# Hybrid diffusion step on one core: the first modulation quarter is loaded right behind the first token tile, and a quarter's projections stand partly ahead of the next quarter's modulation

## The chip, the cores and the metric

The kernel runs on one core of one Trainium2 chip, in one launch. The metric is the device time of one execution in microseconds (us), the median of repeated runs; lower is better.

## The reference, cut to what matters

Two layers (DEPTH 2, D_MODEL 1024) run over 256 latent tokens and 128 context tokens. What matters here is how a layer begins: a conditioning vector is multiplied with a wide weight, the normalised tokens are scaled and shifted by pieces of the product, and one combined projection follows.

```
mod_ctx = (jax.nn.silu(c_ctx) @ w_mod[l] + b_mod[l])[None, :]
mod_lat = jax.nn.silu(c) @ w_mod[l] + b_mod[l]
...
sh1, sc1, g1, sh2, sc2, g2 = [m[:, None, :] for m in jnp.split(mod, 6, axis=-1)]
h = layer_norm(x) * (1 + sc1) + sh1
z = h @ p["w_in"] + p["b_in"]
q, k, v, conv_in, f_in, gates = jnp.split(z, SPLITS, axis=-1)
... attention, convolution and Fourier branches, merged by gates
x = layer_norm(ALPHA * x + g1 * (merged @ p["w_o"]), p["ln1_g"], p["ln1_b"])
... feed-forward with a depthwise convolution, second residual and norm
```

All of it is float32; the kernel keeps that accuracy by splitting an operand into a high and a low float32r part and adding three products.

## The kernel before

The 384 tokens are three tiles of 128: t0 and t1 latent, t2 context. The 1024 features are eight blocks of 128 (k).

**Start.** `run` sets up constants and a run of 30 products of zeros on PE (`busy`, L130), loads the three token tiles (`s`, 512 KB each) and the parameter rows (`par`), normalises the tiles on DVE (L327 and L329 statistics, L330 adds eps, POOL takes the root at L331, L336 applies it), and calls the layers.

**First layer, `start_first` (L415).** Modulation is done in four quarters s, each giving shift and scale for two k blocks. A quarter has two 1024 KB weight blocks (`raw<-w_mod`, L247). Its generator `mod` first loads them, then runs 32 small products in two groups of 16 (L232, 16 for each block), copies the result out of PSUM (L264, DVE), transposes it (L268, PE) and adds the bias into the columns `md` (L277, four small DVE instructions, for shift and scale of context and latents).

With `md` there, `to_hT` transposes two k blocks of each token tile (L356, PE) and applies scale and shift, one block on ACT (L365) and the other on DVE (L363); `split_hT` makes the high part on ACT (L371) and the low part on DVE (L372). The projection weight of the quarter (`s<-w_z`, two halves of 512 KB) is split by `halves` into `whi` on ACT (L178) and `wlo` on DVE (L179). `products` then runs 36 matmuls of 128x512 (L195 to L197): 2 halves, 3 token tiles, 2 k blocks, 3 products each, into six PSUM accumulators. Those of quarter s are traced after the transposes of quarter s + 1 (`late`, L436).

**What sets the order.** Each engine executes its own list in order. The lists are made by a scheduler from the traced program; buffers come from pools whose sizes are in `BUFS` (L80): among them 3 `raw`, 5 `whi`, 5 `wlo`, 8 `s4`, and two PSUM tiles `ps` (L119), which modulation and transposes share. All loads of this stage are issued by SP, on one queue. After `start_first` the convolution's input projection (L474, weights `raw<-w_cv`) begins.

Of the kernel before, what the change touches and what calls it, by code (L numbers as in the profile page):

```python
# [78 lines left out]
class Net:  # L79
# [46 lines left out]
    def busy(self, n):  # L126
        """products of zeros: they keep the tensor engine's clock up until the data is there"""
        ps = self.psum()
        for i in range(n):
            self.nc.tensor.matmul(ps[:, 0:P], self.zeros, self.zeros, start=i == 0, stop=i == n - 1)  # L130
# [39 lines left out]
    def halves(self, parts):  # L170
        """f32 half units -> their float32r (high, low) parts"""
# [11 lines left out]
    def raw(self, w):  # L183
        """one block [P, kn, 2048 // kn] of weights"""
        r = self.t("raw", [P, 2048]).rearrange("p (k c) -> p k c", k=w.shape[1])
        self.load(r, w)
        return r
# [5 lines left out]
    def mm3(self, ps, lh, ll, rh, rl, first, last):  # L193
        mm = self.nc.tensor.matmul
        mm(ps, lh, rh, start=first, stop=False)  # L195
        mm(ps, lh, rl, start=False, stop=False)  # L196
        mm(ps, ll, rh, start=False, stop=last)  # L197

    def ws_tile(self, hT, w, n=NTOK):
        """one 128-column tile of h @ w, features on partitions"""  # L200
# [6 lines left out]
    MODS = {"A": 0, "B": 1, "G": 2}  # L207

    def mod(self, l, kind, s=None):
        """c @ w_mod for the groups of a kind (A: sh1 sc1, B: sh2 sc2, G: g1 g2), or quarter s of them;  # L210
        a step per row tile"""
# [108 lines left out]
    def stats(self, src, w):  # L320
        """columns: mean, 1 / sqrt(var + eps)"""
# [16 lines left out]
    def norm_act(self, dst, src, total):  # L338
        """dst: src normalised, total: its rows' sums"""
# [9 lines left out]
    def to_hT(self, l, which, t, k0, nk, xhat, tag):  # L349
        """modulated transposes of row tiles k0.. of token tile t"""  # L350
# [64 lines left out]
    def start_first(self, l, xhat, hT, z):  # L415
        """first layer: a quarter of the modulation at a time, then what needs it"""
        acc = [[self.psum("acc") for _ in range(3)] for _ in range(2)]
        mods = [self.mod(l, "A", s) for s in range(4)]

        def loads(s):  # L420
            ws = [self.s4().rearrange("p (k c) -> p k c", k=2) for _ in range(2)]
# [4 lines left out]
        def products(s, raws):  # L426
            for half, (hi, lo) in enumerate(self.halves(raws)):
                for t in range(3):
# [6 lines left out]
        next(mods[0])  # L435
        late = None  # L436
        for s in range(4):
            for _ in mods[s]:
                pass
            raws = loads(s)  # L440
            if s < 3:
                next(mods[s + 1])
            for t in range(3):
                self.split_hT(t, 2 * s, 2, self.to_hT(l, 0, t, 2 * s, 2, xhat[t], "ps"), hT, 0)
            if late:
                products(*late)
            late = s, raws
        self.setup_late()
        bb = self.b_bias(l)
        products(*late)  # L450
# [114 lines left out]
    def fourier(self, f):  # L565
        """per channel tile the transform's transpose, split"""
# [33 lines left out]
    def rotate(self, dst, src, t, n):  # L600
        """dst, src: [P, n heads, 2, 32]"""
# [10 lines left out]
    def keys(self, l, z):  # L612
        """transposed keys (columns t0 t1 ctx prompt) of each kv head: high parts twice, low parts twice"""
# [146 lines left out]
    def close(self, acc, x, gate, lg, lb, last=None):  # L760
        """acc: the sub-layer's output for one token tile in two banks; returns the new x and its rows' sums"""
# [32 lines left out]
    def layer(self, l, first, hT, mods):  # L794
# [24 lines left out]
        # feed-forward: the first NF column tiles go by token tile, in plain float32  # L819
# [131 lines left out]
    def run(self):  # L951
        self.setup()
        xhat = [self.s4() for _ in range(3)]
        for t in range(3):
            self.load(xhat[t], self.x_src(0, t))
        self.columns(0)
# [17 lines left out]
def layout(i):  # L974
    """the inputs in the order in which the kernel loads them"""
# [4 lines left out]
    def cols(w, width=256):  # L980
        """[L, R, C] -> per block of columns [P, R / P, width]"""
# [3 lines left out]
    def rows(w, n=2):  # L985
        """[L, R, C] -> per n row tiles [P, n, C]"""
# [54 lines left out]
```

## Time and profile before

| | |
|---|---|
| median of 3 runs | 1193.04 us (1192.70 to 1194.32) |
| span of the profiled execution | 1190.3 us |
| around that span, by the median | 2.7 us |
| PE busy | 1170.9 us, 98% of the span |
| DVE, ACT, POOL busy | 754.0, 523.9, 76.4 us |

The profiled execution's span runs from its first to its last instruction; no other time is given for that execution, so what lies around it is taken as the median less the span. A busy PE is not PE at its peak: matmuls are pipelined, and the next one starts before the one ahead has ended.

### The profile page before, as it was taken

The numbers are of one execution on the slowest core, as the hardware profiler recorded it, in microseconds if no ns is written. First come the engines' busy times: TensorE is split into PE (matmuls) and PEld (weight loads), VectorE is DVE, ScalarE is ACT, GpSimd is POOL, SyncE is SP. The second block draws the span as 40 slices with busy tenths as digits, with TensorE's granted clock in tenths as the row PEclk, the third lists the DMA queues.
The fourth block names the chain that finished last, engine by engine and source line by source line (L and its number), as shares of the span: only waits on it lengthen the run. The fifth ranks groups of instructions, "written<-read, shape, count | busy, mean of one in ns | idle before, by whom it ended". The sixth has DMA issues, their size and how long they took to land.

```text
span 1190.3 us, 16806 instructions
## 1 busy us (share of the span) xinstructions
PE 1170.9 (98%) x6637; PEld 1023.5 (86%) x6637; DVE 754.0 (63%) x1269; ACT 523.9 (44%) x875; POOL 76.4 (6%) x91
## 2 busy tenths in 40 slices
PE   8999999999999999999999999999999999999996
PEld 6788788867899999999966887888989999999995
DVE  6569965424676665566685598653557666655668
ACT  3447643223464443444454566432427444443440
POOL 1010001111100000000011000011211000000001
PEclk9999999999999999999999999999999999999999
DMA  9655576674263333343425545775335343433311
GB/s 374 268 182 185 184 243 235 210 267 164 103 230 124 115 134 130 118 140 108 141 81 187 191 156 193 236 236 175 107 140 200 123 140 107 142 109 139 117 61 53
DMA packets 49791, 194.90 MB, mean 164 GB/s; under 512 B 5760, under 2 KB 6800, under 8 KB 34608
## 3 DMA queue, kind: packets, MB, share of 16 engines
q1 hardware_dynamic: 49280, 193.04, 46.8%
q8 instruction: 52, 0.85, 0.3%
q10 hardware_dynamic: 432, 0.79, 0.2%
q14 instruction: 27, 0.22, 0.1%
HBM read 190.37 MB, written 3.44 MB: 163 GB/s over the span
## 4 chain that ended last, share of the span: by engine, by line
PE 86%; DVE 6%; ACT 2%; DMA 2%; POOL 1%; issue 1%; SPq 0%; POOLq 0%; DVEq 0%; ACTq 0%
PE ps L195 17%; PE ps L196 16%; PE ps L197 16%; PE acc L195 9%; PE acc L196 9%; PE acc L197 8%; PE acc L232 4%; PE acc L716 1%; POOL sm L331 1%; PE acc L704 1%; DVE wlo L179 1%; DVE s L777 1%; DMA raw<-w_mod 1%; DVE sm L327 1%; DVE s L767 1%
## 5 line engine op out<-in xcount | busy, mean ns | idle before, releaser
L179 DVE TENSOR_TENSOR wlo<-raw,whi 128x1024 fp32r<-128x1024 f32 x216 | 269.9, 1251 | 278.7 <-ACT whi L178 278.6
L195 PE MATMUL ps<-hT,whi 128*128 128x386 f32 (+1 forms) x1088 | 372.6, 342 | 0.2 <-ACT g L503 0.2
L196 PE MATMUL ps<-hT,whi 128*128 128x386 f32 (+1 forms) x1088 | 369.1, 339 | 0.0
L197 PE MATMUL ps<-hT,wlo 128*128 128x386 f32 (+1 forms) x1088 | 368.9, 339 | 0.0
L178 ACT CAST whi<-raw 128x1024 fp32r<-128x1024 f32 x216 | 225.7, 1048 | 314.4 <-PE ps L196 217.8
L195 PEld LDWEIGHTS ps<-hT,whi 128*128 128x128 f32 x1088 | 205.2, 189 | 33.2 <-issue 20.3
L196 PEld LDWEIGHTS ps<-hT,whi 128*128 128x128 f32 x1088 | 205.2, 189 | 4.1 <-issue 3.2
L197 PEld LDWEIGHTS ps<-hT,wlo 128*128 128x128 f32 x1088 | 205.3, 189 | 2.7 <-issue 2.7
L196 PE MATMUL acc<-wlo,r 128*128 128x512 f32 x360 | 142.3, 395 | 0.0
L195 PE MATMUL acc<-whi,r 128*128 128x512 f32 x360 | 142.2, 395 | 0.0
L197 PE MATMUL acc<-whi,r 128*128 128x512 f32 x360 | 141.9, 394 | 0.0
L197 PEld LDWEIGHTS acc<-whi,r 128*128 128x128 f32 x360 | 67.6, 188 | 16.3 <-DVE r L899 0.5
L195 PEld LDWEIGHTS acc<-whi,r 128*128 128x128 f32 x360 | 67.6, 188 | 15.1
L196 PEld LDWEIGHTS acc<-wlo,r 128*128 128x128 f32 x360 | 67.6, 188 | 14.5
L734 DVE SCALAR_TENSOR_TENSOR cv<-upad,cst,cv 128x399 f32<-128x399 f32 x120 | 69.9, 625 | 0.1
L898 ACT CAST r<-g 128x386 fp32r<-128x386 f32 x44 | 22.7, 516 | 97.5 <-DVE g L896 97.5
L331 POOL TENSOR_TENSOR sm<-sm,mhalf 128x1 f32<-128x1 f32 x21 | 22.9, 1094 | 613.3 <-DVE sm L330 608.4
L518 POOL TENSOR_TENSOR g<-g,g 128x384 f32<-128x384 f32 x32 | 34.8, 1087 | 393.9 <-DVE g L517 389.7
L875 ACT ACTIVATE g<-ps,cst 128x386 f32<-128x386 f32 x84 | 56.3, 670 | 0.0
L232 PE MATMUL acc<-s,cpad 128*32 128x512 f32 x320 | 55.4, 604 | 0.7 <-DMA s<-w_mod 0.7
L878 DVE SCALAR_TENSOR_TENSOR g<-ps,cst,g 128x385 f32<-128x385 f32 x84 | 52.0, 620 | 2.8
L876 DVE SCALAR_TENSOR_TENSOR g<-ps,cst,g 128x385 f32<-128x385 f32 x84 | 51.6, 614 | 0.3
(184 smaller groups left out, 1314.6 us busy)
## 6 DMA issues: line engine op xcount, KB each, us to landing
raw<-w_u SPq DMA_DIRECT2D x44, 1024.0 KB, 5.0
s<-w_mod SPq DMA_DIRECT2D x160, 256.0 KB, 4.6
raw<-w_g SPq DMA_DIRECT2D x24, 1024.0 KB, 6.8
raw<-w_d SPq DMA_DIRECT2D x22, 1024.0 KB, 4.9
raw<-w_mod SPq DMA_DIRECT2D x8, 1024.0 KB, 12.4
raw<-w_o SPq DMA_DIRECT2D x8, 1024.0 KB, 7.8
s<-w_z SPq DMA_DIRECT2D x8, 512.0 KB, 11.0
raw<-w_cv SPq DMA_DIRECT2D x4, 1024.0 KB
```

The costliest lines, as they stand in the source:

```text
L178: self.nc.scalar.copy(hi, raw)
L179: self.nc.vector.tensor_tensor(lo, raw, f32(hi), op=ALU.subtract)
L195: mm(ps, lh, rh, start=first, stop=False)
L196: mm(ps, lh, rl, start=False, stop=False)
L197: mm(ps, ll, rh, start=False, stop=last)
L232: nc.tensor.matmul(ps[32 * i:32 * i + 32, 0:n], self.cpad[:, k, :], src[k, i], start=k == 0, stop=k == KD - 1)
L331: nc.gpsimd.tensor_tensor(mv[:, 3:4], mv[:, 2:3], self.mhalf, op=ALU.pow)
L518: nc.gpsimd.tensor_tensor(merged[m], merged[m], gt, op=ALU.add)
L734: nc.vector.scalar_tensor_tensor(c, u[:, i:i + CV_W], w, c, op0=ALU.mult, op1=ALU.add)
L875: nc.scalar.activation(c, ps, AF.Identity, bias=cols["ffn_b"][:, i:i + 1], scale=w[1])
L876: nc.vector.scalar_tensor_tensor(c[:, 1:NPAD], ps[:, 0:NPAD - 1], w[0], c[:, 1:NPAD], op0=ALU.mult, op1=ALU.add)
L878: nc.vector.scalar_tensor_tensor(c[:, 0:NPAD - 1], ps[:, 1:NPAD], w[2], c[:, 0:NPAD - 1], op0=ALU.mult, op1=ALU.add)
```

## The change

The first quarter's modulation weights are queued behind token tile t0 and ahead of `par`, the first half of `w_z`, tiles t1 and t2, and the second half of `w_z`. In `start_first` a quarter's weights are loaded ahead of its transposes, and its products are no longer held until the next quarter: the first token tile's products (for the first quarter, the first two tiles') stand ahead of the next quarter's modulation, and the others behind it. `issue_after` queues the PE instructions of the block under it behind the named matmul.

```diff
 def mm3(self, ps, lh, ll, rh, rl, first, last):
...
-        mm(ps, ll, rh, start=False, stop=last)
+        self.last_mm = mm(ps, ll, rh, start=False, stop=last)
...
 def start_first(self, l, xhat, hT, z):
...
-        next(mods[0])
-        late = None
-        for s in range(4):
+        def modulate(s):
             for _ in mods[s]:
                 pass
-            raws = loads(s)
+
+        raws = loads(0)
+        modulate(0)
+        for s in range(4):
             if s < 3:
                 next(mods[s + 1])
+                more = loads(s + 1)
             for t in range(3):
                 self.split_hT(t, 2 * s, 2, self.to_hT(l, 0, t, 2 * s, 2, xhat[t], "ps"), hT, 0)
-            if late:
-                products(*late)
-            late = s, raws
-        self.setup_late()
-        bb = self.b_bias(l)
-        products(*late)
+            ws = self.halves(raws)
+            cut = 1 if s else 2
+            products(s, ws, range(cut))
+            if s < 3:
+                with self.tc.issue_after(self.last_mm.ins):
+                    modulate(s + 1)
+                raws = more
+            else:
+                self.setup_late()
+                bb = self.b_bias(l)
+            products(s, ws, range(cut, 3))
...
 def run(self):
         self.setup()
         xhat = [self.s4() for _ in range(3)]
-        for t in range(3):
+        self.load(xhat[0], self.x_src(0, 0))
+        self.first_mods = [self.mod(0, "A", s) for s in range(4)]
+        next(self.first_mods[0])
+        self.columns(0)
+        self.first_w = [self.s4().rearrange("p (k c) -> p k c", k=2) for _ in range(2)]
+        self.load(self.first_w[0], self.a["w_z"][0, 0, 0])
+        for t in (1, 2):
             self.load(xhat[t], self.x_src(0, t))
-        self.columns(0)
+        self.load(self.first_w[1], self.a["w_z"][0, 1, 0])
```

**DVE, the first quarter.** Before: the rows around the copy of the first modulation product (L264); `s_120` is token tile t2, `s_221` and `s_222` the two halves of the first `w_z`.

```order
L330 TENSOR_SCALAR sm_160<-sm_160 128x1
L336 TENSOR_SCALAR s_120<-s_120,sm_160 128x1024
L264 COPY s_176<-ps_181 128x128
L277 TENSOR_TENSOR md_140<-ps_215,cst_131 128x2 x4
L179 TENSOR_TENSOR wlo_328<-s_221,whi_327 128x1024
L363 TENSOR_SCALAR s_233<-ps_230,md_140 128x128
```

All three tiles are normalised ahead of the copy there. In the changed program the same place reads as follows; `s_119` and `s_120` are tiles t1 and t2, `s_144` the first half of `w_z`.

```order
L179 TENSOR_TENSOR wlo_259<-s_144,whi_258 128x1024
L327 BN_STATS sm_158<-s_119 128x6 x2
L264 COPY s_122<-ps_185 128x128
L329 BN_AGGR sm_161<-sm_158 128x2
L327 BN_STATS sm_166<-s_120 128x6
L330 TENSOR_SCALAR sm_161<-sm_161 128x1
L327 BN_STATS sm_166<-s_120 128x6
L336 TENSOR_SCALAR s_119<-s_119,sm_161 128x1024
L329 BN_AGGR sm_169<-sm_166 128x2
L277 TENSOR_TENSOR md_143<-ps_219,cst_134 128x2
```

A weight split and two statistics now stand ahead of the copy, and the norms of two tiles between the copy and the columns. The list goes on:

```order
L277 TENSOR_TENSOR md_143<-ps_219,cst_134 128x2
L330 TENSOR_SCALAR sm_169<-sm_169 128x1
L277 TENSOR_TENSOR md_143<-ps_219,cst_134 128x2 x2
L336 TENSOR_SCALAR s_120<-s_120,sm_169 128x1024
L277 TENSOR_TENSOR md_143<-ps_219,cst_134 128x2
L179 TENSOR_TENSOR wlo_263<-s_145,whi_262 128x1024
L363 TENSOR_SCALAR s_237<-ps_234,md_143 128x128
```

The last of the four L277, which completes the columns, has moved behind the norm of t2.

**PE, from the first quarter to the second.** Before: the transposes of quarter 1 (L356 into `ps_303`, `ps_311`) stand between products of quarter 0.

```order
L268 MATMUL ps_288<-ident,s_225 128x128
L356 MATMUL ps_303<-ident,s_118 128x128 x2
L195 MATMUL acc_173<-whi_331,hT_165 128x512
L196 MATMUL acc_173<-wlo_332,hT_165 128x512
L197 MATMUL acc_173<-whi_331,hT_166 128x512
L356 MATMUL ps_311<-ident,s_119 128x128 x2
L195 MATMUL acc_173<-whi_331,hT_165 128x512
```

In the changed program all three pairs stand behind the last product of quarter 0, and the first product that needs them right behind.

```order
L195 MATMUL acc_184<-whi_262,hT_174 128x512
L196 MATMUL acc_184<-wlo_263,hT_174 128x512
L197 MATMUL acc_184<-whi_262,hT_175 128x512
L356 MATMUL ps_351<-ident,s_118 128x128 x2
L356 MATMUL ps_359<-ident,s_119 128x128 x2
L356 MATMUL ps_367<-ident,s_120 128x128 x2
L195 MATMUL acc_179<-whi_375,hT_174 128x512
```

No product of the old quarter is left to stand among the transposes; the same holds at the two later quarters.

**ACT, before the last quarter.** Before: `whi_612` and `whi_616` are the last quarter's `w_z`, `s_535` the first scaled block, `whi_683` a `w_cv` weight of the next stage.

```order
L178 CAST whi_612<-s_528 128x1024
L365 ACTIVATE s_535<-ps_532,md_140 128x128
L178 CAST whi_616<-s_529 128x1024
L365 ACTIVATE s_543<-ps_540,md_140 128x128
L371 CAST hT_165<-s_535 128x2x128
```

In the changed program three splits of the next stage's weights stand ahead of the last quarter's scaling.

```order
L178 CAST whi_683<-raw_681 128x1024
L178 CAST whi_687<-raw_681 128x1024
L178 CAST whi_839<-raw_837 128x1024
L365 ACTIVATE s_579<-ps_576,md_143 128x128
L365 ACTIVATE s_587<-ps_584,md_143 128x128
L371 CAST hT_174<-s_579 128x2x128
```

The first L365 of that quarter has moved behind `whi_839`, whose DVE part (L179) likewise stands ahead of the quarter's first L363.

## Rows read from the trace of the kernel before

**Rows 1.** The page, busy time and share of the span by engine.
```profile
PE 1170.9 (98%) x6637; PEld 1023.5 (86%) x6637; DVE 754.0 (63%) x1269; ACT 523.9 (44%) x875; POOL 76.4 (6%) x91
```
**Rows 2.** Busy time by stretches: stretch, length, then busy (count) by engine.
```profile
core 0: us, PE busy (x) PEld busy (x) DVE busy (x) ACT busy (x) POOL busy (x), PEclk, DMA share, GB/s
13.77:18.34 4.57, 2.48 (x40) 1.53 (x40) 3.64 (x10) 3.26 (x6) 0.00 (x0) 1.00 1.02 420
18.34:62.00 43.66, 43.66 (x362) 33.92 (x363) 25.72 (x54) 18.02 (x32) 3.13 (x6) 1.00 0.79 303
```
**Rows 3.** Timeline of the start: start, us, engine, instruction, idle before and releaser.
```profile
1.05 9.70 PE L130 MATMUL ps<-zeros 128*128 128x128 f32 x60 [1.05 <-DVE zeros L135]
4.75 0.69 DVE L327 BATCH_NORM_STATS2 sm<-s 128x6 f32<-128x512 f32 x1 [2.09 <-DMA s<-x_s]
...
8.72 2.08 DVE L336 TENSOR_SCALAR s<-s,sm 128x1024 f32<-128x1024 f32 x2
...
13.17 0.55 POOL L331 TENSOR_TENSOR sm<-sm,mhalf 128x1 f32<-128x1 f32 x1 [3.63 <-DVE sm L330]
13.75 0.81 DVE L336 TENSOR_SCALAR s<-s,sm 128x1024 f32<-128x1024 f32 x1 [0.66 <-POOL sm L331]
...
13.77 1.08 PE L232 MATMUL ps<-raw,cpad 128*32 128x128 f32 x32 [1.27 <-DMA raw<-w_mod]
...
14.92 0.29 DVE L264 COPY s<-ps 128x128 f32<-128x128 f32 x1 [0.36 <-PE ps L232]
15.03 1.04 ACT L178 CAST whi<-s 128x1024 fp32r<-128x1024 f32 x1 [10.94 <-DMA s<-w_z]
...
15.63 0.36 DVE L277 TENSOR_TENSOR md<-ps,cst 128x2 f32<-128x2 f32 x4 [0.42 <-PE ps L268]
...
16.11 1.23 DVE L179 TENSOR_TENSOR wlo<-s,whi 128x1024 fp32r<-128x1024 f32 x1
...
17.25 0.72 DVE L363 TENSOR_SCALAR s<-ps,md 128x128 f32<-128x128 f32 x2
...
17.88 0.40 ACT L371 CAST hT<-s 128x256 fp32r<-128x256 f32 x1
...
18.34 0.50 PE L195 MATMUL acc<-whi,hT 128*128 128x512 f32 x1 [0.18 <-ACT hT L371]
```
**Rows 4.** Timeline of quarter 2: DVE waits while work behind its head is ready.
```profile
31.60 1.05 ACT L178 CAST whi<-s 128x1024 fp32r<-128x1024 f32 x1 [1.31 <-DMA s<-w_z]
...
34.45 0.29 DVE L264 COPY s<-ps 128x128 f32<-128x128 f32 x1 [3.67 <-PE ps L232]
...
35.70 1.21 DVE L179 TENSOR_TENSOR wlo<-s,whi 128x1024 fp32r<-128x1024 f32 x1
```
**Rows 5.** Timeline of quarter 2: transposes among products, and the scaling behind them.
```profile
35.22 0.38 PE L356 MATMUL ps<-ident,s 128*128 128x128 f32 x2
35.36 0.48 PE L196 MATMUL acc<-wlo,hT 128*128 128x512 f32 x1
...
35.88 0.46 ACT L365 ACTIVATE s<-ps,md 128x128 f32<-128x128 f32 x1 [3.23 <-DVE md L277]
```
**Rows 6.** Timeline of PE around one group of modulation products.
```profile
32.98 0.39 PE L195 MATMUL acc<-whi,hT 128*128 128x512 f32 x1
33.30 1.08 PE L232 MATMUL ps<-raw,cpad 128*32 128x128 f32 x32
34.31 0.51 PE L196 MATMUL acc<-wlo,hT 128*128 128x512 f32 x1
34.65 0.39 PE L197 MATMUL acc<-whi,hT 128*128 128x512 f32 x1
34.88 0.39 PE L195 MATMUL acc<-whi,hT 128*128 128x512 f32 x1
```
**Rows 7.** Busy time by stretches, the products of zeros and the end of PE's work.
```profile
1.05:4.00 2.95, 2.95 (x14) 2.95 (x15) 0.21 (x1) 1.50 (x2) 0.51 (x2) 1.00 0.55 167
6.80:10.60 3.80, 3.80 (x35) 3.76 (x34) 3.73 (x8) 0.00 (x0) 1.90 (x4) 1.00 1.05 428
1180.00:1185.00 5.00, 1.12 (x5) 0.57 (x3) 4.62 (x9) 0.00 (x0) 0.65 (x1) 0.94 0.28 105
```

More of the change, by code (lines that the diff above doesn't have):

```diff
@@ L417, in start_first @@
         acc = [[self.psum("acc") for _ in range(3)] for _ in range(2)]
-        mods = [self.mod(l, "A", s) for s in range(4)]
+        mods = self.first_mods
         def loads(s):
+            if s == 0:
+                return self.first_w
             ws = [self.s4().rearrange("p (k c) -> p k c", k=2) for _ in range(2)]
@@ L424, in loads, with products @@
             return ws
-        def products(s, raws):
-            for half, (hi, lo) in enumerate(self.halves(raws)):
-                for t in range(3):
+        def products(s, ws, tiles):
+            for half, (hi, lo) in enumerate(ws):
+                for t in tiles:
                     ts = slice(t * P, t * P + P)
@@ L953, in run @@
         xhat = [self.s4() for _ in range(3)]
-        for t in range(3):
+        self.load(xhat[0], self.x_src(0, 0))
[5 more added lines that the diff above has]
+        for t in (1, 2):
             self.load(xhat[t], self.x_src(0, t))
-        self.columns(0)
+        self.load(self.first_w[1], self.a["w_z"][0, 1, 0])
         for x in xhat:
```

## The prediction

> **What bounds the kernel now.** I read the page's busy shares first, then PE's busy time by stretches, then the timeline of the first 62 us, engine by engine. PE is busy for 1170.9 of 1190.3 us [rows 1], so only what makes PE start later or stand still moves the end. From 18.34 to 62 us PE is busy for 43.66 of 43.66 us [rows 2]: from its first projection on, the start stage has no hole at all. In the 4.57 us before that it is busy for 2.48 [rows 2]. What can be won therefore lies ahead of 18.34 us, at most a few microseconds. What can be lost is larger: every hole opened behind 18.34 us is paid in full, since PE's 19.4 idle microseconds of the whole span are too few and too scattered to give it back.
>
> **The way to the first product, before.** The second block of the first modulation weights lands at 13.7 us (L232 starts at 13.77, released by a DMA), the copy L264 follows at 14.92, the four L277 end at 15.63 + 0.36 = 15.99, and the first product starts at 18.34, that is 2.35 us later, behind an L179, an L363 and an L371 [rows 3]. So it is transfer, PE, DVE, ACT, PE in turn.
>
> **The same way after.** Transfers land in the order of SP's queue. Token tile t0 is there at 4.7 us; from there to 13.7 us the other two tiles, `par` and two modulation blocks land, 1.0 + 0.25 + 2.0 = 3.25 MB in 9.0 us, or 2.77 us a MB [rows 3]; half a MB more (first `w_z`) takes until 15.03, the same rate. In the new order the modulation blocks (2.0 MB) land at 4.7 + 5.5 = 10.2, `par` at 10.9, the first half of `w_z` at 12.3, t1 at 13.7, t2 at 15.1. PE's products of zeros last until 1.05 + 9.70 = 10.75 [rows 3] as before, then `par` is transposed, and the two groups L232 end at about 13.6 instead of 14.85. That is the 1.2 us which the edit wins.
>
> It is lost on DVE, whose list puts other work ahead of the copy. L178 needs `w_z` (12.3) and 1.04 us, so L179 runs from 13.4 to 14.6; the two statistics of t1 start 0.6 apart (0.69 each), and L264 comes at 15.85, 0.9 later than 14.92. Behind it stand two statistics of t2 (until 17.3), the root on POOL (0.55, with hand-over 0.7), L336 of t1 (0.81, done about 18.3), then again a root and L336 of t2, done at 20.1 (each duration from [rows 3]). The last L277 follows, ending at 20.2 instead of 15.99. The old 2.35 us with L179, L363 and L371 in them follow it, less 0.3 since ACT has no L178 between: the first product starts at about 22.25 instead of 18.34. **First term: +3.9 us.** Bounds: +2.9 if transfers land early enough never to hold DVE (the list alone then costs 1.0 less), +4.5 if the two L336 cost 1.04 each, as the pair of 2.08 did beside POOL's work [rows 3].
>
> That DVE cannot pass the copy forward is in the trace: in quarter 2 `whi` is ready at 32.65, yet its L179 starts at 35.70, behind an L264 that DVE awaited for 3.67 us with nothing else to do [rows 4].
> The Trainium skill, "TensorE: Matmul & The Clock Gate", section "Architectural detail: the array is 16× 32×32, not 1× 128×128", states that ACT and DVE take their work strictly first in, first out. By that rule the sum here stands; by its opposite the copy would run at 13.7 and the change would win. The trace agrees with the rule.
>
> **The three later quarters.** Before, the transposes stand among old products, each pair followed by a product 0.14 us later [rows 5], and PE never waits. After, the last old product (start T) is followed by the three pairs and then by products that need their result. In numbers from rows: a pair takes 0.24 of PE. ACT's two L365 (0.46 each, [rows 5]) start at T + 0.7, the first L363 at T + 1.2 since it writes the same tile behind ACT, taking 0.4; L371 (0.40) ends at T + 2.05 [rows 3]. The third pair has to wait as well, for one of only two `ps` tiles. The first new product starts at T + 2.15. Less the old product's 0.23 and three pairs (0.72), which PE has to do in any case, that is a hole of 1.2 us for quarter 1.
> Quarter 2: an L178 (1.04) stands on ACT between the L365 and the L371, shifting most of it: hole 1.9.
> Quarter 3: ACT has an L178 of the next stage ahead of its first L365. It takes the fifth `whi` buffer, free only when the last product of quarter 2 has read it, so it starts at T + 0.45. L365 then comes at T + 1.5, DVE does that weight's L179 (1.23) until T + 2.75, L363 to 3.1, L371 to 3.55, product at T + 3.6: hole 2.7. Queued behind that waiting L178 are all scalings of the last quarter, and PE waits for them.
> **Second term: +5.8 us** (1.2 + 1.9 + 2.7). Bounds: 4.0 if the splits between happen to run during the old products (1.2 + 1.3 + 1.5), 7.0 if each L365 and L371 meets one more split part-way.
>
> **Small terms.** A group of L232 among products costs 0.32 ahead instead of 0.23, and 0.34 behind it instead of 0.23 [rows 6], 0.2 in all. Quarters 1 to 3 have five groups apart before and three after: **-0.4 us**. The work itself is the same: equal counts of products, transposes and splits. SP is moved past nothing that PE awaits: with its queue at 8.3 us a quarter (3 MB at 2.77) and PE at about 12, weight blocks land some microseconds ahead; a block of quarter 2 now waits for the buffers of quarter 1's modulation, read at about 28.5 (22.25, 24 products of 0.23 and a group's half), and would land about 33.5, needed near 37. If that cover went, the hole would be up to 1 us. The later stages start with the same data and the same lists but for local swaps; I cost them at nothing, hidden beside PE.
>
> **The clock.** Between 13.6 and 22.25 us PE would have only L268 and three pairs of transposes, about 1 us of work, with one stretch of some 3.7 us wholly idle. The trace shows what idling does: PE's last product ends at 1181.12 and the granted clock of 1180 to 1185 is 0.94, so it fell to half 0.6 us before the end of that stretch, at 1184.4, 3.3 us after the work [rows 7]. It shows a start at half as well: 14 passes of the zeros in 2.95 us against 35 in 3.80 later, 0.21 against 0.11 us each, up to 6.8 us, that is 5.75 us after PE's first [rows 7]. If the clock falls to 1.2 GHz ahead of 22.25 us, the products after it run at half rate for a while; 5.75 us of that lose 2.9. Bounds 0 and +2.9; I take **+2.5**, near the row of the start, a little less since transposes run just ahead.
> The Trainium skill, "TensorE: Matmul & The Clock Gate", section "Part 1: The HAM clock gate (the "warmup" mystery)", calls half speed the default that activity lifts. By that rule this term counts; without it the sum is the first rival's below. The trace agrees where it shows a fall, but has no stretch like the new one.
>
> **Sum.** 3.9 + 5.8 - 0.4 + 2.5 = +11.8 us. On the span of 1190.3 that gives 1202.1, with the 2.7 around it 1204.8, the same as 1193.04 + 11.8.
>
> **Rivals.**
> *The clock stays up* (27%). The 0.5 us of transposes every few microseconds may keep it. Before, 2.48 busy in 4.57 us did; against it stands the far emptier stretch. Then +9.3, 1202.3 us.
> *Only the start is late* (9%). If splits and scalings of quarters 1 to 3 run while old products still run, as they do before, the holes vanish: 3.9 - 0.4 = +3.5, 1196.5. Against it: the transposes themselves stand behind the last product.
> *The early modulation is worth it* (9%). The place is DVE's list between 13 and 20 us: were the two tiles' norms not in the way of the columns, L277 would end at 14.8, the first product start at 17.1, and with -0.4 and late holes hidden by products kept back (the two tiles held behind modulation) the time would be 1193.0 - 1.2 - 0.4 = 1191.4; with first products also unbroken, 1190.3. It decides if L264 starts before 14.5 and L277 ends before 15.9. For it speaks PE's 1.2 us; against it the order of DVE's rows.
>
> **How the numbers follow.** The forecast has 55%. Low: 2.9 + 4.0 - 0.4 = +6.5, 1199.5, a little under for landings; high: 4.5 + 7.0 - 0.4 + 2.9 = +14.0, 1207.0, and 1 for the uncovered block. The range 1199.0 to 1208.0 holds the forecast and the first rival with their bounds and leaves out the other two, 18%. About 0.2%, 2.4 us, can be told from no change by a measurement of this kernel. Slower by more: 0.55 + 0.27 + 0.09 = 0.91; the last rival is split, within 0.05 and faster 0.04.
>
> **What would show it.** In the changed profile: L264 of the first quarter near 15.9 and the last L277 near 20.2; the first L195 near 22; PE holes of 1 to 3 us at the three quarter ends, near 33, 46 and 59 us, released by DVE or ACT; the stretch in which PE has no hole, up to 62 us before [rows 2], interrupted, and the stage's end 9 to 12 us later; passes twice as long for some microseconds behind 22 us if the clock fell. The prediction is wrong if the first product starts before 19 us, or if PE shows no hole from there on.

## The result and the profile after

| | before | after |
|---|---|---|
| median | 1192.79 us (5 runs, 1191.07 to 1194.32) | 1203.74 us (5 runs, 1202.71 to 1203.93) |
| span of the profiled execution | 1190.3 us | 1200.9 us (its own time 1202.71) |
| first projection product starts | 18.34 us | 21.60 us |
| last of the 144 products of the start stage starts | 61.27 us | 71.82 us |

The ratio is 1.0091, with a 95% interval of 1.0078 to 1.0103. The forecast was 1204.8 us in a range of 1199.0 to 1208.0. The last row of the table says where to look: the 10.6 us by which the start stage ends later are the 10.6 us by which the span is longer. On balance nothing is lost behind it and nothing is given back (in between the difference drifts down to 10.1 and up again). One of the eleven runs of the last experiment below was disturbed (1640.67 us at a mean clock of 0.654) and is left out of its range. The last product of the stage, before and after:

```profile
61.27 0.40 PE L197 MATMUL acc<-whi,hT 128*128 128x512 f32 x1
```
```profile
71.82 0.39 PE L197 MATMUL acc<-whi,hT 128*128 128x512 f32 x1
```

The page of the changed kernel, busy time by engine, answers to [rows 1]:

```profile
PE 1173.3 (98%) x6637; PEld 1025.8 (85%) x6637; DVE 755.4 (63%) x1269; ACT 524.7 (44%) x875; POOL 75.6 (6%) x91
```

The counts are those of before to the instruction. By the page's shares alone the two kernels are the same. The difference appears by stretches; the first two rows below answer to [rows 2] (stretch, length, then busy time and count by engine, granted clock, DMA share, GB/s), the others are short stretches around the start and around the last quarter's end:

```profile
13.21:21.60 8.39, 1.92 (x20) 0.90 (x9) 7.62 (x20) 2.37 (x4) 1.10 (x2) 0.74 1.02 413
18.34:62.00 43.66, 36.96 (x324) 28.39 (x324) 21.89 (x47) 17.02 (x30) 0.40 (x1) 0.93 0.80 300
```
```profile
17.00:20.00 3.00, 0.20 (x1) 0.23 (x2) 2.46 (x9) 0.26 (x1) 0.55 (x1) 0.54 1.00 412
...
22.00:24.00 2.00, 2.00 (x6) 1.52 (x6) 1.17 (x4) 1.53 (x4) 0.00 (x0) 0.50 1.07 440
24.00:26.00 2.00, 2.00 (x10) 1.65 (x9) 1.35 (x2) 1.62 (x2) 0.00 (x0) 0.98 0.96 393
...
61.00:62.00 1.00, 0.03 (x1) 0.03 (x1) 1.00 (x3) 0.10 (x2) 0.00 (x0) 0.82 1.15 442
62.00:65.00 3.00, 3.00 (x8) 2.37 (x9) 1.83 (x5) 1.51 (x4) 0.00 (x0) 0.50 0.92 350
```

Before the first product PE is busy for 1.92 of 8.39 us, and in the stretch that had no hole before for 36.96 of 43.66. The column of the granted clock (the third number from the right) shows two places at 0.5, that is at the lower of its two levels, 1.2 GHz: from about 17 to 24 us and from about 61.7 to 65 us. A full busy column at half clock carries fewer products: 6 in two microseconds against 10 in the next two.

The timeline of the start, which answers to [rows 3] (start, length, engine, instruction, idle time before and what ended it):

```profile
12.98 1.23 DVE L179 TENSOR_TENSOR wlo<-s,whi 128x1024 fp32r<-128x1024 f32 x1
...
14.12 1.28 DVE L327 BATCH_NORM_STATS2 sm<-s 128x6 f32<-128x512 f32 x2
...
15.32 0.27 DVE L264 COPY s<-ps 128x128 f32<-128x128 f32 x1
...
15.65 0.33 PE L268 MATMUL ps<-ident,s 128*128 128x128 f32 x1 [2.17 <-DVE s L264]
...
16.99 0.81 DVE L336 TENSOR_SCALAR s<-s,sm 128x1024 f32<-128x1024 f32 x1
...
18.77 0.81 DVE L336 TENSOR_SCALAR s<-s,sm 128x1024 f32<-128x1024 f32 x1 [0.53 <-POOL sm L331]
19.50 0.15 DVE L277 TENSOR_TENSOR md<-ps,cst 128x2 f32<-128x2 f32 x1
...
19.80 0.66 PE L356 MATMUL ps<-ident,s 128*128 128x128 f32 x2 [3.60 <-DVE md L277]
...
21.60 0.79 PE L195 MATMUL acc<-whi,hT 128*128 128x512 f32 x1
...
24.23 0.39 PE L195 MATMUL acc<-whi,hT 128*128 128x512 f32 x1
```

The last row is the seventh product. The copy L264 of the modulation product stands behind a weight split and two statistics, and the last L277 behind two tiles' norms. PE has finished the modulation product early and then waits 2.17 and 3.60 us for DVE.

The timeline of the last quarter's end, which answers to [rows 5], shows the largest of the three holes. ACT's L178 and DVE's L179 on `raw` prepare weights of the next stage:

```profile
58.86 0.39 PE L197 MATMUL acc<-whi,hT 128*128 128x512 f32 x1
...
59.09 0.60 PE L356 MATMUL ps<-ident,s 128*128 128x128 f32 x4
...
59.29 1.05 ACT L178 CAST whi<-raw 128x1024 fp32r<-128x1024 f32 x1 [1.75 <-PE acc L197]
...
60.24 0.80 ACT L365 ACTIVATE s<-ps,md 128x128 f32<-128x128 f32 x2
60.37 1.23 DVE L179 TENSOR_TENSOR wlo<-raw,whi 128x1024 fp32r<-128x1024 f32 x1 [1.57 <-ACT whi L178]
61.51 0.72 DVE L363 TENSOR_SCALAR s<-ps,md 128x128 f32<-128x128 f32 x2
61.95 0.41 ACT L371 CAST hT<-s 128x256 fp32r<-128x256 f32 x1 [0.91 <-DVE s L363]
61.97 0.69 PE L356 MATMUL ps<-ident,s 128*128 128x128 f32 x2 [2.28 <-DVE s L363]
...
62.41 0.80 PE L195 MATMUL acc<-whi,hT 128*128 128x512 f32 x1
...
65.10 0.40 PE L195 MATMUL acc<-whi,hT 128*128 128x512 f32 x1
```

Read it from the product at 62.41 upwards (the one at 65.10 is the seventh of its quarter): the first product of the new quarter waits for L371, that for L363, that for DVE's L179, that for ACT's L178, and this one was released by PE's last reader of an old weight buffer. Four hand-overs stand between two products that were neighbours before.

The two smaller holes, from one timeline: the first, between the last product of quarter 0 and the first of quarter 1, has a single wait, and the second has two, since an L178 stands on ACT ahead of the L371:

```profile
33.17 0.39 PE L197 MATMUL acc<-whi,hT 128*128 128x512 f32 x1
...
34.78 0.44 PE L356 MATMUL ps<-ident,s 128*128 128x128 f32 x2 [0.78 <-DVE s L363]
...
35.21 0.50 PE L195 MATMUL acc<-whi,hT 128*128 128x512 f32 x1
...
45.64 0.40 PE L197 MATMUL acc<-whi,hT 128*128 128x512 f32 x1
...
47.00 1.04 ACT L178 CAST whi<-s 128x1024 fp32r<-128x1024 f32 x1
47.26 0.44 PE L356 MATMUL ps<-ident,s 128*128 128x128 f32 x2 [0.78 <-DVE s L363]
...
48.40 0.50 PE L195 MATMUL acc<-whi,hT 128*128 128x512 f32 x1 [0.70 <-ACT hT L371]
```

### The profile page after: what moved, and what is told of

It reads as the page before. It is cut to its first block, busy times and chain, and to the rows that moved or that the text cites. A ratio compares the mean times of both kernels' runs of the same rounds, so it can differ in the third digit from the quotient of the medians.

```text
span 1200.9 us, 16796 instructions
## 1 busy us (share of the span) xinstructions
PE 1173.3 (98%) x6637; PEld 1025.8 (85%) x6637; DVE 755.4 (63%) x1269; ACT 524.7 (44%) x875; POOL 75.6 (6%) x91
## 4 chain that ended last, share of the span: by engine, by line
PE 87%; DVE 7%; ACT 2%; POOL 1%; DMA 1%; issue 1%; POOLq 0%; DVEq 0%; SPq 0%; ACTq 0%
PE ps L195 16%; PE ps L196 16%; PE ps L197 16%; PE acc L195 9%; PE acc L196 9%; PE acc L197 8%; PE acc L232 4%; DVE wlo L179 1%; PE acc L725 1%; POOL sm L331 1%; DVE sm L327 1%; PE acc L713 1%; DVE s L786 1%; PE ps L130 1%; DVE s L776 1%
## 5 line engine op out<-in xcount | busy, mean ns | idle before, releaser
L179 DVE TENSOR_TENSOR wlo<-raw,whi 128x1024 fp32r<-128x1024 f32 x216 | 269.9, 1252 | 288.3 <-ACT whi L178 283.5
L178 ACT CAST whi<-raw 128x1024 fp32r<-128x1024 f32 x216 | 225.6, 1047 | 322.0 <-PE ps L196 220.3
L232 PE MATMUL acc<-s,cpad 128*32 128x512 f32 x320 | 55.4, 604 | 0.7 <-DMA s<-w_mod 0.7
```

The costliest lines, as they stand in the source:

```text
L178: self.nc.scalar.copy(hi, raw)
L179: self.nc.vector.tensor_tensor(lo, raw, f32(hi), op=ALU.subtract)
L232: nc.tensor.matmul(ps[32 * i:32 * i + 32, 0:n], self.cpad[:, k, :], src[k, i], start=k == 0, stop=k == KD - 1)
```

## The experiments

The kernel before was timed again beside the experiments: 1193.84 us beside the first four, 1193.04 beside the next four, 1192.71 beside the last. Ratios are taken against these. The changed kernel's 1203.74 us were taken beside 1192.79, so a difference from the changed kernel can be off by about a microsecond; where it matters, the distance of each kernel from its own before is given too.

**The loads alone.** The new order of the loads in `run`, with `start_first` as it was before (products held until the next quarter's transposes stand); the diff shows how that function differs from before.

```diff
 def start_first(self, l, xhat, hT, z):
-        mods = [self.mod(l, "A", s) for s in range(4)]
+        mods = self.first_mods
         def loads(s):
+            if s == 0:
+                return self.first_w
...
-        next(mods[0])
```

> The new order of loads with the products as before the change (held until the next quarter's transposes). Theory A, the start and the later holes are two separate losses: the first product starts at about 22 us instead of 18.3 and the clock falls before it, but from there on PE has no hole: +3 to +5 us, 1196 to 1198. Rival B, one loss only, the late start costs nothing by itself since transfers bound the stage anyway: within 1 us of 1192.8. Rival C, the late start brings the later holes with it: 1202 to 1204 as with the whole change.

Measured: 1195.68 us (10 runs), ratio 1.0019 (1.0010 to 1.0029). The waits of PE in the start stage (waiting operand and line, what released it, total, times, longest):

```profile
PE ps L356 <- DVE md L277: 3.6, 1, 3.6
PE ps L268 <- DVE s L264: 2.4, 1, 2.4
...
```

The waits of the start are all there (the one left out is of 0.7, at 21.18), and none behind it: the holes belong to the other half of the change. The time is 1.8 us above the kernel before, under the 3 to 5 expected, and the first product starts at 23.66 instead of the expected 22, since products of quarter 1's modulation (L232 at 21.80) stand ahead of it on PE. The stage's 144th product starts at 65.09, 3.8 us later than before, and the clock is at half around the first product here as well (0.52 on average from 17.5 to 24.5 us).

**The order alone.** The new `start_first`, with the loads in the order of before.

```diff
 def run(self):
-        self.load(xhat[0], self.x_src(0, 0))
+        for t in range(3):
+            self.load(xhat[t], self.x_src(0, t))
+        self.columns(0)
...
-        for t in (1, 2):
-            self.load(xhat[t], self.x_src(0, t))
```

> The loads in the order of before the change, with the new order of products (first tile ahead of the next quarter's modulation, transposes behind the last old product). Theory A, two separate losses: first product at 18.3 as before the change, then holes of about 1.1, 1.8 and 2.6 us at the three quarter ends and the clock falling in the last: +5 to +7 us, 1198 to 1200. Rival B, the holes come of the late start alone: within 1 us of 1192.8.

Measured: 1197.23 us (6 runs), ratio 1.0030 (1.0018 to 1.0041), 3.4 us above the kernel before where 5 to 7 were expected. The three holes are there, but two things at the start were not expected. The first product starts at 19.35, 1.0 later than before: its L371 stands on ACT behind an L178 that awaits the second half of `w_z` (until 17.95). And the granted clock is down around it, though the loads are in the old order:

```profile
17.00:23.00 6.00, 4.33 (x11) 3.12 (x12) 3.75 (x8) 2.81 (x6) 0.00 (x0) 0.50 1.02 415
```

In the third hole, where the fall was expected, it stays at 1.00. So in this execution the start loses too, with the loads where they were; whether that comes of the order or of the one execution stays open. The third hole is shorter than in the changed kernel, since only one split of the next stage stands in it, behind the scaling and ahead of L371:

```profile
57.80 1.04 ACT L178 CAST whi<-raw 128x1024 fp32r<-128x1024 f32 x1
...
59.20 0.50 PE L195 MATMUL acc<-whi,hT 128*128 128x512 f32 x1 [0.70 <-ACT hT L371]
```

The 144th product starts at 67.46, 6.2 later than before. With the 3.8 of the loads alone that makes 10.0 of the 10.6 us, so by the traces the two halves of the change nearly add up. By the medians they do not (1.8 and 3.4 against 10.9). Three things bear on the gap, none of them measured by itself. The loads alone give a microsecond back behind the stage (their span is 2.8 us longer, not 3.8). The traced execution of the order alone is the slowest of its six (1198.32). And the profiled execution of before is one without a fall of the clock (mean 0.998), while its other runs on that chip have means of 0.995 to 0.997, so the median of before contains some of what the edits are charged with; the experiment with zeros in the kernel before bears on this.

**The norms behind the columns.** The changed kernel, with the statistics and norms of t1 and t2 queued on DVE behind the last of the four L277.

```diff
 def mod(self, l, kind, s=None):
-                nc.vector.tensor_tensor(dst, part, bias, op=ALU.add)
+                self.last_md = nc.vector.tensor_tensor(dst, part, bias, op=ALU.add)
...
 def start_first(self, l, xhat, hT, z):
+        with self.tc.issue_after(self.last_md.ins):
+            for x in xhat[1:]:
+                self.norm(x, x, D)
...
 def run(self):
-        for x in xhat:
-            self.norm(x, x, D)
+        self.norm(xhat[0], xhat[0], D)
```

> The changed kernel with the statistics and norms of token tiles t1 and t2 queued on DVE behind the four L277 of the first quarter; the same work in all. Theory A, the order of DVE's list makes the start late: columns ready near 15.5 instead of 19.65, products start near 17 and go on, 3 us and the first fall of the clock (1.2 us) are won back: 1199 to 1200. Rival B, the amount of DVE work that is left once t1 and t2 land late (four statistics, two norms, two splits, about 7 us) makes it late whatever its order: the first product starts near 17, but PE stands again until t1 is normalised and the stage ends at most 1 us earlier: 1202.5 to 1203.7.

Measured: 1206.06 us (4 runs, 1200.90 to 1207.47), ratio 1.0095 (1.0071 to 1.0118): no gain, and above what either theory allowed. The columns are there 4.5 us earlier, and the time goes elsewhere:

```profile
14.80 0.36 DVE L277 TENSOR_TENSOR md<-ps,cst 128x2 f32<-128x2 f32 x4 [0.42 <-PE ps L268]
...
17.20 1.04 ACT L178 CAST whi<-s 128x1024 fp32r<-128x1024 f32 x1 [1.49 <-DMA s<-w_z]
...
18.60 0.79 PE L195 MATMUL acc<-whi,hT 128*128 128x512 f32 x1 [3.62 <-ACT hT L371]
...
20.91 0.81 DVE L336 TENSOR_SCALAR s<-s,sm 128x1024 f32<-128x1024 f32 x1 [0.44 <-POOL sm L331]
...
21.64 0.41 DVE L363 TENSOR_SCALAR s<-ps,md 128x128 f32<-128x128 f32 x1
...
23.31 0.80 PE L195 MATMUL acc<-whi,hT 128*128 128x512 f32 x1 [0.84 <-ACT hT L371]
```

The first product now stands behind an L178 that awaits its weights. The next tile's scaling (the L363 at 21.64) stands on DVE behind the norm of the tile after it (L336), and the product at 23.31 waits for that. The work of two norms has to be done between the landing of t1 and t2 and their products, whichever end of it the columns stand at. PE's waits up to the product at 23.31 add up to 5.7 us (1.22, 3.62 and 0.84), where the changed kernel has 6.5 (2.17, 3.60 and 0.70): the theory that the order of DVE's list alone costs the 3.3 us falls. That the stage ends 2.4 us later than in the changed kernel (144th product at 74.21) has other places in this trace: the clock is at 0.50 from 17 to 26.5 us and on average at 0.57 from 50 to 54, and the second hole has waits of 1.76 and 1.16 us where the changed kernel has 0.78 and 0.70. The fastest of the four executions (1200.90, mean clock 0.996, the highest of the four) lies 2.8 below the changed kernel; it was not traced.

**The splits behind the last scaling.** The changed kernel, with the next stage's `w_cv` splits queued on ACT behind the last quarter's last L371; DVE's L179 of them follow.

```diff
 def split_hT(self, t, k0, nk, h3, hT, gap):
-        self.nc.scalar.copy(hs, h3)
+        self.last_split = self.nc.scalar.copy(hs, h3)
...
+        self.first_split = self.last_split
...
-                for j, w in enumerate(self.halves(self.col_halves(self.raw(a["w_cv"][l, u])))):
+                raw = self.raw(a["w_cv"][l, u])
+                if l == 0:
+                    with self.tc.issue_after(self.first_split.ins):
+                        ws = self.halves(self.col_halves(raw))
+                else:
+                    ws = self.halves(self.col_halves(raw))
+                for j, w in enumerate(ws):
```

> The changed kernel with the splits of the next stage's first weights queued on ACT behind the last quarter's last L371. Theory A, the third hole is long because an L178 that waits for a buffer, and its L179, stand ahead of the scaling: the hole shrinks from 2.6 to about 1.1 us, PE idles less than 1 us at a time and the clock does not fall at 61.6 (six products at 0.23 instead of 0.43, 1.3 us): -2.5 to -3 us, 1200.7 to 1201.3. Rival B, the two ps tiles make it long: no change, 1203.7. Rival C, the hole shrinks but the clock falls all the same: -1.5, 1202.2.

Measured: 1200.70 us (4 runs, 1200.47 to 1201.49), 3.0 below the changed kernel, as expected. The third hole, and the clock over it:

```profile
59.14 0.39 PE L197 MATMUL acc<-whi,hT 128*128 128x512 f32 x1
...
61.19 0.50 PE L195 MATMUL acc<-whi,hT 128*128 128x512 f32 x1
```
```profile
59.00:62.50 3.50, 2.72 (x15) 1.82 (x14) 1.93 (x5) 2.31 (x7) 0.00 (x0) 1.00 0.46 185
62.50:66.00 3.50, 3.50 (x17) 2.85 (x16) 3.40 (x5) 2.91 (x4) 1.48 (x2) 1.00 0.02 5
```

From 59.14 to 61.19 is 2.05, where the changed kernel has 3.55 from 58.86 to 62.41, and the clock stays at 1.00. So the splits cost 1.5 us of waiting, and the six products behind take 1.49 us (61.19 to 62.68) instead of 2.69, another 1.2 us, which are the clock's. The stage ends 2.4 earlier (its 144th product starts at 69.41), a little less than the two together. The 3.0 are the difference of two medians taken beside different runs of the kernel before; over their own before the changed kernel lies 10.95 us and this one 6.86, which would be 4.1. The trace decides what the edit is worth in the stage, and it says 2.4.

**Products of zeros in the start gap.** The changed kernel, with 28 products of zeros on PE while it waits for DVE (`last_mod` and `last_tr` name the last L232 and the last transpose).

```diff
+        def fill(n, behind):
+            with self.tc.issue_after(behind.ins):
+                for i in range(n):
+                    self.nc.tensor.matmul(acc[0][0][:, 0:P], self.zeros, self.zeros, start=i == 0, stop=i == n - 1)
...
         modulate(0)
+        fill(8, self.last_mod)
...
-                self.split_hT(t, 2 * s, 2, self.to_hT(l, 0, t, 2 * s, 2, xhat[t], "ps"), hT, 0)
+                h3 = self.to_hT(l, 0, t, 2 * s, 2, xhat[t], "ps")
+                if s == 0 and t < 2:
+                    fill((16, 4)[t], self.last_tr)
+                self.split_hT(t, 2 * s, 2, h3, hT, 0)
```

> The changed kernel with 28 products of zeros in TensorE's idle stretches before the first product (8 behind the last L232, 16 behind token tile t0's transposes, 4 behind t1's), into an accumulator whose first real product starts it anew; nothing else is changed. Theory A, the granted clock falls at 17.27 us because TensorE stood nearly idle from 13.5 us on, and the fall costs the 1.24 us that the first six products lose: the clock stays up until the third hole, the six products take 0.23 us each instead of 0.43, and the time is 1.0 to 1.4 us less, 1202.3 to 1202.8 us. The fall in the third hole (61.64 us) should stay. Theory B, the fall is a consequence of something else (the waiting itself, or a fixed time after the start): the clock falls as before and the time stays within 0.5 us of 1203.7. Theory C, the zeros get in the way of the transposes: the first product starts later than 21.6 and the time rises.

Measured: 1201.43 us (5 runs, 1199.82 to 1202.35), ratio to before 1.0066 (1.0054 to 1.0079), 2.3 below the changed kernel and more than expected. The stretches of the start:

```profile
17.00:20.00 3.00, 2.97 (x28) 2.81 (x27) 2.39 (x10) 0.08 (x1) 0.67 (x2) 1.00 1.02 421
20.00:24.00 4.00, 3.94 (x22) 3.04 (x23) 3.11 (x7) 3.05 (x7) 0.00 (x0) 1.00 1.03 418
```

The clock stays at 1.00, and the first six products take 1.50 us (21.77 to 23.27) instead of 2.63 (21.60 to 24.23). That is 1.1 us; 0.2 of it goes into the later first product. The last quarter adds nothing to it in this trace: its hole is as long as in the changed kernel (3.55 from 57.85 to 61.40), the clock is at half behind it (0.50 from 62.5 to 65.5), and the stage ends only 0.6 earlier, at 71.19. The two profiled executions are 1.1 us apart (1201.63 and 1202.71); the rest of the 2.3 is mostly that the changed kernel's median lies 1.0 above its profiled execution. Two of the five runs have a mean clock of 0.998 (the profiled one has 0.997) and are the fastest (1199.82 and 1200.08). That the second fall was missing in these two is inferred from their means; they were not traced.

**Splits behind and zeros, together.** The two edits shown last, in one kernel.

> The changed kernel with both edits: the next stage's weight splits queued on ACT behind the last quarter's L371, which took 3.0 us off, and the 28 products of zeros in the start gap. Theory A, the losses are separate terms: no fall of the clock is left in the start stage, and the time is that of the splits alone, 1200.7, less 1.0 to 1.4, so 1199.3 to 1199.7 us; what remains over the kernel before, 6.5 to 7 us, is the first product's 3.3 us and three holes of 1.1 to 1.8. Theory B, the clock's fall only moves (it falls in the first hole behind quarter 0 instead): 1200.2 to 1201.2 us.

Measured: 1198.50 us (5 runs, 1198.02 to 1198.79), ratio 1.0044 (1.0032 to 1.0057). The mean clock is 0.997 or 0.998 in all runs, and no fall is left in the profiled start stage. Its 144th product starts at 67.96, 6.7 us later than before: 3.3 for the first product and the three holes of about 1.1, 1.8 and 1.1, less some half a microsecond that before itself loses among its first products. Against the splits alone the zeros take 2.2 us off by the medians, more than was expected, and 1.4 by the two traces (their 144th products start at 69.41 and 67.96). The difference is that of the kernel before, which was 0.8 us slower beside the splits alone: over their own before the two kernels lie 6.9 and 5.5 us, 1.4 apart, as expected. The runs lie closer together than those of any other kernel here.

**Only t2 moved.** A version of the early modulation on the kernel before: t0 and t1 ahead of `par` and the modulation weights as before, t2 behind both halves of the first `w_z`, its norm on DVE behind the low parts of t0 and t1, and quarter 0's products of t0 and t1 ahead of t2's transposes. The later quarters hold their products as before; quarter 1's weight splits are queued behind its columns (L277), which the diff leaves out. `turn` stands for the transposes, scaling and parts of the named tiles; the diff is against the kernel before.

```diff
 def start_first(self, l, xhat, hT, z):
+        modulate(0)
+        ws = self.halves(loads(0))
+        next(mods[1])
+        turn(0, range(2))
+        with self.tc.issue_after(self.last_low.ins):
+            self.norm(xhat[2], xhat[2], D)
+        products(0, ws, range(2))
+        with self.tc.issue_after(self.last_mm.ins):
+            turn(0, [2])
+        modulate(1)
...
 def run(self):
-        for t in range(3):
+        for t in range(2):
             self.load(xhat[t], self.x_src(0, t))
         self.columns(0)
+        self.first_mods = [self.mod(0, "A", s) for s in range(4)]
+        next(self.first_mods[0])
+        self.first_w = [self.s4().rearrange("p (k c) -> p k c", k=2) for _ in range(2)]
+        self.load(self.first_w[0], self.a["w_z"][0, 0, 0])
+        self.load(self.first_w[1], self.a["w_z"][0, 1, 0])
+        self.load(xhat[2], self.x_src(0, 2))
-        for x in xhat:
+        for x in xhat[:2]:
             self.norm(x, x, D)
```

> A version of the early modulation on the kernel before: tiles t0 and t1 are loaded and normalised ahead, then par and the first modulation weights, both halves of the first w_z, and only then t2, whose norm stands on DVE behind the low parts of t0 and t1 (L372); a quarter's products are held behind the next quarter's transposes as before, but in the first quarter those of t0 and t1 stand ahead of t2's transposes. Theory A, the early modulation loses only because two tiles' norms fall between its product and its columns: with one tile moved and its norm behind, L264 starts at 13.5 and the first product at 16.9 to 17.2 (1.2 to 1.4 us ahead of 18.34), no hole follows, and the time is 1191.4 to 1191.8. Theory B, the transfers set the pace of quarter 1 whatever comes first: TensorE gains 1.3 us at the start and stands still as long before the first product of quarter 1 (its w_z lands at 23.3 and 24.7 in either order), and the time is 1192.5 to 1194.

Measured: 1191.35 us (11 runs, 1189.76 to 1194.05), ratio 0.9986 (0.9977 to 0.9994): by the medians faster than before by 1.7 us. The stretches of the start, up to the 144th product:

```profile
13.33:17.09 3.76, 1.23 (x18) 0.52 (x7) 2.85 (x9) 3.26 (x6) 0.00 (x0) 0.99 1.05 424
17.09:20.50 3.41, 3.41 (x8) 2.73 (x9) 3.12 (x7) 0.25 (x1) 0.14 (x1) 0.51 1.00 413
20.50:61.48 40.98, 40.98 (x352) 32.03 (x351) 23.37 (x51) 17.38 (x30) 4.85 (x6) 1.00 0.76 293
```

L264 starts at 13.67 and the first product at 17.09, 1.25 earlier than before, and PE has no hole behind it, so quarter 1's transfers do not set the pace. But the clock is at half right at the first product, and the 1.2 us won are lost again among the first products: in this trace the 144th starts at 61.48, 0.2 later than before. The span is nevertheless 0.9 us shorter (1189.4): 0.6 us come in the stage that follows, up to 112 us (PE waits 1.0 us there instead of 1.5), and the rest later. So this trace does not show the 1.7 us as a gain of the start, and the cause of the shorter waits behind it stays open.

**Zeros in the start gap of the kernel before.** Six products of zeros (2 behind the first quarter's last L232, 4 behind t1's transposes), by the same `fill`.

> The kernel before with 6 products of zeros in its start gap (2 behind the last L232 of the first quarter, 4 behind t1's transposes). Its profiled run shows the clock at full speed throughout (mean 0.998), but other runs of it have 0.995 to 0.997. Theory A, in those runs the clock falls in the stretch from 14.85 to 18.34 us, and the products of zeros keep it up: the clock is 0.998 in all runs and the median falls by 0.5 to 1.5 us, to 1192.3 to 1193.3 against 1193.8 on this chip. Theory B, their lower clock has another place (a later stage): no change beyond 0.3 us.

Measured: 1191.91 us (11 runs, 1191.18 to 1193.35) against 1193.04, ratio 0.9990 (0.9981 to 0.9999). The gain of 1.1 us is at the edge of what can be told. The means of the clock are 0.996 to 0.998 where before has 0.994 to 0.997 on that chip. They rise, but not to 0.998 in all runs, so part of its lower clock has another place, which was not looked for. The trace cannot settle it either: the clock of the start is at 1.00 in both profiled executions, and the first product starts 0.4 earlier here because the second modulation block landed earlier (L232 at 13.08 instead of 13.77). That the zeros made this gain is not shown.

**t2 moved, and zeros.** Both of the last two: 2 products of zeros behind the last L232, 8 behind t1's transposes.

> The version with only t2 moved, with 10 products of zeros in its start gap (2 behind the last L232 of the first quarter, 8 behind t1's transposes). Its run without them had the clock at half from 17.02 to 20.43 us, right at its first product at 17.09, and its six first products took 0.43 us each where the later ones take 0.23. Theory A, the zeros keep the clock up and both gains add: the six products give back 1.2 us, so 1191.35 - 1.2 = 1190.1, between 1189.8 and 1190.6 us, some 2.5 to 3 under the kernel before. Theory B, the first products then only wait for the low parts (L372, 17.90 and later) or for quarter 1's weights, and the 1.2 us turn into a wait: 1190.8 to 1191.4 us.

Measured: 1190.14 us (11 runs, 1189.70 to 1190.74), ratio 0.9978 (0.9969 to 0.9987). This is the version that beats both kernels, by 2.6 us against before and 13.6 against the changed one. Its stretches answer to [rows 2]:

```profile
13.77:17.34 3.57, 3.25 (x30) 2.85 (x26) 2.85 (x9) 3.26 (x6) 0.00 (x0) 1.00 1.04 421
17.34:62.00 44.66, 44.66 (x370) 35.28 (x371) 28.25 (x60) 18.76 (x32) 6.75 (x7) 1.00 0.80 311
```

The first product starts 0.25 us later than without zeros, and the seventh 1.0 earlier (18.83 instead of 19.81). The theory that the saved time turns into a wait falls. The 144th product starts at 60.22, 1.0 us earlier than before and 1.3 earlier than without zeros. That is what the start gives; the span is 2.1 us shorter than before, and the other 1.0 comes behind the stage, 0.6 of it up to 112 us as in the version without zeros.

## Why the prediction was right, and which of its terms were off

- **The first product: forecast +3.9, measured +3.3.** The mechanism is the forecast one: L264 at 15.32 (15.85 forecast), the last L277 ending at 19.65 (20.2), the first product 1.95 behind that (2.05). The half microsecond is a landing: the first half of `w_z` was there at 11.9, not 12.3, so the split and the statistics on DVE stood earlier. That it is the amount of norm work and not merely its place in the list, the run with the norms behind the columns showed: it only brought PE's waits at the start from 6.5 to 5.7 us.
- **The three holes: forecast 1.2, 1.9 and 2.7, measured 1.1, 1.8 and 2.6.** These come from the starts of the last old and the first new product (2.04, 2.76 and 3.55 apart), less the 0.23 and 0.72 of PE's own work, as the forecast did. The run of the splits behind shows the third one's cause.
- **The clock: forecast one fall costing 2.5, measured two of about 1.2 to 1.3 each.** This is the step that failed, by place. From the first product to the seventh it is 2.63 us, where six at 0.23 take 1.4 (and 1.50 in the run with zeros). The forecast let the low clock last 5.75 us of products; it came down earlier, at about 17 us, and most of its time fell on a PE that was waiting anyway. The second fall, in the third hole, was not forecast at all: the products from 62.41 to 65.10 take 2.69 instead of 1.4. That the sum came out at 2.5 is chance. The mean clock of the profiled executions shows the two falls as well, 0.993 against 0.998. The forecast's 5.75 us were read off slow passes of zeros in [rows 7], whose row gives a granted clock of 1.00; the trace has no record of the clock ahead of 6.80 us, and the column shows 1.00 where there is none. So that this start ran at half clock is argued from the passes and not shown by the column.
- **Groups of L232: forecast -0.4.** Not measured by itself. Before lost 0.5 us among its own first six products, which start 0.32 apart instead of 0.23, as some of them waited for their high and low parts; the forecast had left that out. The terms measured, 3.3 + 5.5 + 2.5 - 0.5 = 10.8, are 0.2 more than the 10.6 found, which leaves about -0.2 for these groups and whatever else there is.
- **The cover for the weight blocks held**: no wait of PE in the start stage is for a transfer.
- **The rivals.** *The clock stays up*: it fell in every profiled run of the new loads or the new order that had no zeros. *Only the start is late*: that is what the loads alone do; with the whole change the three holes came too. *The early modulation is worth it*: not as it was built, since L264 started at 15.32 and L277 ended at 19.65, where 14.5 and 15.9 were to decide. It is true in another form: with one tile moved instead of two, its norm where PE has products to run, and the clock kept up by zeros, the stage ends 1.0 us earlier than before.

The Trainium skill, "TensorE: Matmul & The Clock Gate", section "Part 1: The HAM clock gate (the "warmup" mystery)", says that the throttled state is the default and activity releases it. The trace agrees in a form that can be used: products of zeros, which compute nothing, kept the clock at 1.00 through 8 us of waiting, from 13.4 to 21.8 us.

## What to carry to other kernels

Before a transfer is moved forward, follow what it feeds to the first product, and look at what stands on each engine's list between them: data that lands late brings its own work (here two norms on DVE), and it falls into the chain that was to be shortened. When products no longer stand among the next step's transposes, each step's hand-overs become a hole, and weight splits of a later stage may queue into it. A nearly idle TensorE of some microseconds often cost its wait here and then about a microsecond again in slow products; if the wait has to be, products of zeros into an accumulator that is not yet in use take the second part away.

## What was not expected of the hardware

The granted clock fell in the third hole of the changed kernel (0.82 in 61 to 62 us, 0.50 behind), where PE had been idle for 2.28 us after four transposes of 0.60 us, and not in the other two holes, with waits of 0.78 and of 0.78 and 0.70. In the version with only t2 moved it fell with a wait of 1.79 us just ahead, after some 4 us with few instructions. The same wait did not always do the same. In the run with the norms behind, PE idles for 2.28 us after the same four transposes ahead of the last quarter, and the clock stays at 1.00 through that hole and behind it (62.45 to 69 us). In the run with zeros in the start gap the hole is the same again, and the clock falls behind it, at about 62.3, when PE has been running products for 0.9 us. By the runs' means the falls also seem to vary between executions of one kernel: the run with the norms behind spread over 6.6 us in four executions (mean clock 0.990 to 0.996), while the one with splits behind and zeros, which leaves no such stretch at the start, spread over 0.8. So a part of what looks like measurement scatter of a kernel can be the clock at one or two places; the executions that would show it were not traced.
